# Hybrid encoder layer on one core: where two kinds of work of the recurrence stand (a PSUM bank, and the engine of the set-aside key update)

## Chip, core and metric

The kernel runs on one core of a Trainium2 chip, in float32 throughout. The metric is the device time of one execution in microseconds (us). Engines are named as in the profile: PE (TensorE, with PEld for its weight loads), DVE (VectorE), ACT (ScalarE), POOL (GpSimd) and SP (SyncE, which issues the DMAs).

## What is computed

One encoder layer over 1024 positions of width 1024: a projection into nine parts, a bidirectional gated recurrence (HGRN2) beside a gated spatial mixer, their merge, a SwiGLU feed-forward part and a gated embedding. The change lies in the recurrence. For each of 8 heads (key and value width 128), forward and backward in time, the reference computes

```python
f = lb + (1.0 - lb) * jax.nn.sigmoid(zf)
k = (1.0 - lb) * jax.nn.sigmoid(-zf)
# S_t = diag(f_t) S_{t-1} + k_t v_t^T,   o_t = S_t^T q_t
o = rms_norm(o_fwd + o_bwd, norm_g)
return o * jax.nn.silu(zg)
```

## The kernel before, in words

The layer is a sequence of stages. The stage of the change lies between about 540 and 1040 us of the profiled execution. Before it come the projections that need no recurrence, behind it the merge of both branches, the output projection, the feed-forward part and the gated embedding.

For each head three functions are called. `proj(h)` multiplies the two forget projections (L133, 96 matmuls of 128x512 for each head, in passes of split float32) and makes from them the gates `F` and the keys `X` and `Y` on ACT (L591 to L598), with a clamp on DVE (L599). `scores(h)` builds the 128x128 score blocks within each of the 8 chunks of 128 positions by doubling: seven levels with blocks of m = 1, 2, 4, ..., 64. `outputs(h)` carries the state from chunk to chunk and adds both directions. The loop calls scores(h), then proj(h+1), then outputs(h). Behind the scores of the last head it issues the last gate projections and the loads for the merge, ahead of outputs(7).

Keys of both directions share two tiles. At a level, `X` holds the keys that this level's matmuls use (of one direction in even blocks, of the other in odd ones), and `Y` holds the others, set aside. A level does the following, with g the half of the 1024 positions:

- L624: 4 matmuls (8 PE instructions in the trace) of X against the decayed queries QA into a bank with the tag "sc", for g = 0 and then g = 1.
- L633, `update`: QA of this half is multiplied by gates (DVE, 128x512).
- L636, `update`: half of the new X2 is made as X times gates (DVE, 128x256 for each g).
- L657: the other half of X2 is copied from Y (ACT, 128x512, one for a level).
- L660: the places in Y that were copied are refilled with X times gates (POOL, 128x512, one for a level). The copy of the next level reads what it wrote. **This is the instruction that the change moves.**
- L643 or L646, `merge`: the scores are taken into SC (ACT for m of 32 and 64, under a mask on DVE below that).
- L666: the gates of the next level are products of neighbours (DVE, 128x1024 at m = 1 down to 128x16 at m = 64).

X, Y and F never read a result of PE. Their chain can run ahead of the matmuls as far as the three buffers of X allow, and in the trace it does: when the matmuls of a head are at m = 64, L636, L657 and L660 are at m = 1 and m = 2 of the next head, and L666 is a head ahead.

`outputs(h)` first builds the states. For two groups of chunks (4, then 3) and in each for both directions d (0 forward, 1 backward) it transposes the keys on PE (L683, 4 or 3 of them) into one PSUM bank, copies them to `kt` on ACT (L685, two buffers), multiplies them with the values (L688, bank "st") and adds the products to the running state S on DVE (L692 for the first, L694 for the others). Then, for each half, it sums scores and states into a bank with the tag "o" (L712), normalises (squares at L715 on ACT, a power on POOL at L101, a scaling at L719 on ACT), transposes into the bank "tr" (L722) and multiplies by the gate on DVE (L724).

PSUM has 8 banks: "mm" 3, "sc" 2, and one each of "tr", "st" and "o". So the transposed keys of both directions go through the one bank "tr" before, and each group waits until ACT has copied the one ahead of it. Only backward groups of the last head go to "sc".

The order on each engine's queue is not written out by hand. The kernel is built under `tile.TileContext(nc, schedule_with_timeline_sim=True)`, which orders the instructions of each engine by its own model of their times, and inserts the waits. On the chip the queues are then fixed: an instruction that waits holds up what stands behind it on its engine. So PE interleaves the matmuls of scores(h), outputs(h-1) or outputs(h), and proj(h+1).

Of the kernel before, what the change touches and what calls it, by code (L numbers as in the profile page):

```python
# [22 lines left out]
H = 8  # L23
# [12 lines left out]
def kernel(ctx: ExitStack, tc: tile.TileContext, a: dict, out: bass.AP):  # L36
# [7 lines left out]
    nc = tc.nc  # L44
# [10 lines left out]
    def ps_tile(tag):  # L55
        return psum.tile([P, NH], F32, name=f"ps_{tag}", tag=tag, bufs=PS_BUFS[tag])
# [16 lines left out]
    def t2(pool, role, bufs=2):  # L73
        return pool.tile([P, NH], F32, name=role, tag=role, bufs=bufs)

    def sm(role, w=1):
        return small.tile([P, w], F32, name=role, tag=role)
# [377 lines left out]
    for t in range(NT):  # L455
        tp = ps_tile(("tr", "o")[t % 2])
# [100 lines left out]
    def view(t, off, dims):  # L557
        tv = t[:]
        return bass.AP(tv.tensor, tv.offset + off, [list(tv.ap[0])] + dims)
# [41 lines left out]
    def scores(h, s):  # L601
        q, X, Y, F = s.q, s.X, s.Y, s.F
        QA = hg.tile([P, 2, T], F32, name="QA", bufs=2)
        ks = hg.tile([P, T], F32, name="ks")
        SC = hg.tile([P, NT, P], F32, name="SC", bufs=2)
        nc.vector.tensor_tensor(out=QA, in0=view(q, 0, [[0, 2], [1, T]]), in1=F, op=ALU.mult)
        nc.vector.tensor_tensor(out=ks, in0=X, in1=Y, op=ALU.add)

        for g in range(2):
            sp = ps_tile("sc")  # L610
            for i in range(4):
                cs = slice((4 * g + i) * P, (4 * g + i + 1) * P)
                nc.tensor.matmul(sp[:, i * P:(i + 1) * P], lhsT=ks[:, cs], rhs=q[:, cs], start=True, stop=True)
            nc.scalar.activation(SC[:, 4 * g:4 * g + 4], sp.rearrange("p (c t) -> p c t", c=4), AF.Copy)

        for li, m in enumerate(LEVELS):
            nb = T // m
            cb = P // (2 * m)

            def level(g):  # L620
                sp = ps_tile("sc")
                for i in range(4):
                    c = 4 * g + i
                    nc.tensor.matmul(  # L624
                        sp[:, i * P:(i + 1) * P], lhsT=X[:, c * P:(c + 1) * P],
                        rhs=view(QA, c * P, [[2 * m, cb], [T + m, 2], [1, m]]), start=True, stop=True)
                return sp

            def update(g, X2):

                o, of = g * NH, g * nb // 2
                qd = [[T + m, 2], [2 * m, nb // 4], [1, m]]
                nc.vector.tensor_tensor(out=view(QA, o, qd), in0=view(QA, o, qd),  # L633
                                        in1=view(F, of + 1, [[nb - 1, 2], [2, nb // 4], [0, m]]), op=ALU.mult)
                dims = [[4 * m, nb // 8], [3 * m, 2], [1, m]]
                nc.vector.tensor_tensor(out=view(X2, o, dims), in0=view(X, o, dims),  # L636
                                        in1=view(F, nb + of + 1, [[4, nb // 8], [1 - nb, 2], [0, m]]), op=ALU.mult)

            def merge(g, sp):
                if m >= 32:  # L640
                    for p0 in range(0, P, m):
                        c0 = p0 ^ m
                        nc.scalar.activation(SC[p0:p0 + m, 4 * g:4 * g + 4, c0:c0 + m],  # L643
                                             sp.rearrange("p (c t) -> p c t", c=4)[p0:p0 + m, :, c0:c0 + m], AF.Copy)
                    return
                nc.vector.copy_predicated(  # L646
                    SC[:, 4 * g:4 * g + 4], masks[:, li, None, :].broadcast_to([P, 4, P]),
                    sp.rearrange("p (c t) -> p c t", c=4))

            X2 = hg.tile([P, T], F32, name="X", bufs=3)  # L650
            sp0 = level(0)
            update(0, X2)
            merge(0, sp0)
            sp1 = level(1)

            mid = [[4 * m, nb // 4], [1, 2 * m]]
            nc.scalar.activation(view(X2, m, mid), view(Y, m, mid), AF.Copy)  # L657
            update(1, X2)
            mid = [[4 * m, nb // 4], [m, 2], [1, m]]
            nc.gpsimd.tensor_tensor(out=view(Y, m, mid), in0=view(X, m, mid),  # L660
                                    in1=view(F, 0, [[4, nb // 4], [nb + 3, 2], [0, m]]), op=ALU.mult)
            X = X2
            merge(1, sp1)
            F2 = hg.tile([P, 2, nb // 2], F32, name=f"F{2 * m}", bufs=2 if m == 64 else 1)
            Fv = F.rearrange("p d (b h) -> p d b h", h=2)
            nc.vector.tensor_tensor(out=F2, in0=Fv[:, :, :, 0], in1=Fv[:, :, :, 1], op=ALU.mult)  # L666
            F = F2
        s.QA, s.SC, s.X, s.Y, s.F = QA, SC, X, Y, F

    def outputs(h, s):  # L670
        QA, SC, X, Y, F, v = s.QA, s.SC, s.X, s.Y, s.F, s.v

        S = hg.tile([P, 2, NT - 1, P], F32, name="S")
        orders = [list(range(NT - 1)), list(range(NT - 1, 0, -1))]
        prev = [None, None]
        for g0 in range(0, NT - 1, 4):
            for d in range(2):
                cs = orders[d][g0:g0 + 4]
                n = len(cs)
                tp = ps_tile("sc" if h == H - 1 and d else "tr")  # L680
                for i, c in enumerate(cs):
                    src = X if c % 2 == d else Y
                    nc.tensor.transpose(tp[:, i * P:(i + 1) * P], src[:, c * P:(c + 1) * P], ident)  # L683
                kt = hg.tile([P, 4, P], F32, name="kt", bufs=2)
                nc.scalar.activation(kt[:, 0:n], tp[:, 0:n * P].rearrange("p (c t) -> p c t", c=n), AF.Copy)  # L685
                up = ps_tile("sc" if h == H - 1 and d else "st")
                for i, c in enumerate(cs):
                    nc.tensor.matmul(up[:, i * P:(i + 1) * P], lhsT=kt[:, i], rhs=v[:, c], start=True, stop=True)  # L688
                for i, c in enumerate(cs):
                    uv = up[:, i * P:(i + 1) * P]  # L690
                    if prev[d] is None:
                        nc.vector.tensor_copy(S[:, d, c - d], uv)  # L692
                    else:
                        nc.vector.scalar_tensor_tensor(  # L694
                            out=S[:, d, c - d], in0=S[:, d, prev[d] - d], scalar=F[:, 1 - d, c:c + 1], in1=uv,
                            op0=ALU.mult, op1=ALU.add)
                    prev[d] = c


        for g in range(2):  # L700
            op = ps_tile("sc" if h == H - 1 and g else "o")
            ssq = sm("os", 4)
            for i in range(4):
                c = 4 * g + i
                cs = slice(c * P, (c + 1) * P)
                terms = [(SC[:, c], v[:, c])]
                if c > 0:
                    terms.append((QA[:, 1, cs], S[:, 0, c - 1]))
                if c < NT - 1:
                    terms.append((QA[:, 0, cs], S[:, 1, c]))  # L710
                for j, (l, r) in enumerate(terms):
                    nc.tensor.matmul(op[:, i * P:(i + 1) * P], lhsT=l, rhs=r, start=(j == 0), stop=(j == len(terms) - 1))  # L712
            on = t2(t1, "on")
            for i in range(4):
                nc.scalar.activation(on[:, i * P:(i + 1) * P], op[:, i * P:(i + 1) * P], AF.Square,  # L715
                                     accum_out=ssq[:, i:i + 1])
            r = rstd_from("o", ssq, 4, 1.0 / P)
            for i in range(4):
                nc.scalar.activation(on[:, i * P:(i + 1) * P], op[:, i * P:(i + 1) * P], AF.Identity, scale=r[:, i:i + 1])  # L719
            tp = ps_tile("tr")  # L720
            for i in range(4):
                nc.tensor.transpose(tp[:, i * P:(i + 1) * P], on[:, i * P:(i + 1) * P], ident)  # L722
            gs = slice(g * NH, (g + 1) * NH)
            nc.vector.scalar_tensor_tensor(out=on, in0=tp, scalar=vec[:, 2, h:h + 1], in1=s.zg[:, gs],  # L724
                                           op0=ALU.mult, op1=ALU.mult)
            if h == H - 1:
                A = (A0, A1)[g]
                split_into(A[0][1][:, h % 4, :], A[1][1][:, h % 4, :], on)
            else:
                nc.sync.dma_start(at_d[h, :, gs], on)  # L730
# [363 lines left out]
```

## Time and profile before

| | us |
|---|---|
| median of 3 runs (1967.69 to 1969.16) | 1967.95 |
| profiled execution, its own time | 1966.99 |
| profiled execution, span from first to last instruction | 1965.2 |
| PE busy in the span | 1910.8 |
| DVE, ACT, POOL busy | 1120.0, 757.2, 206.7 |

The profiled execution is 0.96 us below the median, and 1.8 us of it lie outside its span. Matmuls are pipelined and overlap, so a busy time of PE contains the fill of the engine. Idle time of an engine is put down to what ended it last. The granted clock is full (0.997 in the mean) throughout.

### The profile page before, as it was taken

The page shows a single profiled execution, that of the slowest core. Times are in us where ns is not written, and L with a number is a line of the kernel's source. Part 1 is how long each engine was busy: PE and PEld are TensorE (multiplying, and loading weights), DVE is VectorE, ACT ScalarE, POOL GpSimd, SP SyncE. Part 2 cuts the span into 40 slices and gives each one's busy share as a digit, 9 for nine tenths or more (in the row PEclk, how much of TensorE's full clock was granted, in tenths as well). Part 3 has the DMA queues.
Part 4 walks back from the last instruction along what each step waited for, and adds up shares of the span by engine and source line. Part 5 has one row for each costly group of instructions (what it writes and reads, how often), then busy time and mean ns, then how long its engine had stood idle before and what let it go on. Part 6 is the DMA issues. An engine that isn't in the chain of part 4 may idle for free.

```text
span 1965.2 us, 24005 instructions
## 1 busy us (share of the span) xinstructions
PE 1910.8 (97%) x9264; PEld 1596.0 (81%) x9264; DVE 1120.0 (57%) x1712; ACT 757.2 (39%) x1424; POOL 206.7 (11%) x153
## 2 busy tenths in 40 slices
PE   7999999999999999999989998999999999999999
PEld 6887888888887888888877887888888888888887
DVE  7402385544348777777665468855554537545743
ACT  6312254343354545545441356433333324112321
POOL 2600000000012222222112100000000000001000
PEclk9999999999999999999999999999999999999999
DMA  7220245323231221212336333232222106315222
GB/s 292 93 88 27 87 172 170 130 105 110 86 123 33 70 71 63 66 55 68 126 106 208 107 99 103 97 112 78 89 76 86 65 33 209 108 65 163 92 102 79
DMA packets 82690, 201.86 MB, mean 103 GB/s; under 512 B 8720, under 2 KB 18064, under 8 KB 82576
## 3 DMA queue, kind: packets, MB, share of 16 engines
q1 hardware_dynamic: 82576, 200.33, 30.2%
q8 instruction: 73, 1.20, 0.3%
q14 instruction: 41, 0.34, 0.0%
HBM read 147.35 MB, written 52.95 MB: 102 GB/s over the span
## 4 chain that ended last, share of the span: by engine, by line
PE 90%; DVE 4%; ACT 2%; DMA 2%; POOL 1%; issue 1%; SPq 0%; DVEq 0%; POOLq 0%; ACTq 0%
PE ps_mm L133 29%; PE ps_mm L278 20%; PE ps_sc L133 11%; PE ps_sc L278 10%; PE ps_st L133 6%; PE ps_sc L624 4%; PE ps_o L278 2%; PE ps_o L712 2%; PE ps_tr L278 2%; PE ps_st L278 1%; DVE QA L633 1%; POOL Y L660 1%; PE ps_st L688 1%; ACT SC L643 0%; DMA raw<-in_w_gate_dram 0%
## 5 line engine op out<-in xcount | busy, mean ns | idle before, releaser
L278 PE MATMUL ps_mm<-T,w 128*128 128x512 f32 x1296 | 309.6, 389 | 0.0
L278 PEld LDWEIGHTS ps_mm<-T,w 128*128 128x128 f32 x1296 | 243.2, 188 | 50.7 <-ACT u L228 0.2
L115 DVE TENSOR_TENSOR whl<-raw,whl 128x1024 fp32r<-128x1024 f32 (+1 forms) x70 | 89.6, 1282 | 142.7 <-ACT whl L114 142.6
L660 POOL TENSOR_TENSOR Y<-X,F 128x512 f32<-128x512 f32 x56 | 92.4, 1651 | 696.1 <-DVE F L599 392.4
L624 PE MATMUL ps_sc<-QA,X 128*128 128x128 f32 x896 | 126.4, 288 | 16.9 <-DVE QA L633 16.9
L115 DVE TENSOR_TENSOR w<-sums,w 128x1024 fp32r<-128x1024 f32 x72 | 88.0, 1223 | 94.2 <-ACT w L114 94.2
L624 PEld LDWEIGHTS ps_sc<-QA,X 128*128 128x128 f32 x896 | 116.1, 192 | 26.1 <-DVE QA L633 19.0
L133 PE MATMUL ps_mm<-whl,act 128*128 128x512 f32 x528 | 134.1, 389 | 0.0
L114 ACT ACTIVATE whl<-raw 128x1024 fp32r<-128x1024 f32 (+1 forms) x78 | 79.1, 1017 | 120.2 <-PE ps_sc L133 52.4
L633 DVE TENSOR_TENSOR QA<-QA,F 128x512 f32<-128x512 f32 x112 | 91.8, 828 | 49.2 <-PE ps_sc L624 48.1
L133 PE MATMUL ps_mm<-hTb,whl 128*128 128x512 f32 x480 | 118.6, 396 | 0.0
L133 PEld LDWEIGHTS ps_mm<-whl,act 128*128 128x128 f32 x528 | 99.1, 188 | 20.7
L133 PE MATMUL ps_mm<-hTa,whl 128*128 128x512 f32 x480 | 115.1, 392 | 0.0
L114 ACT ACTIVATE w<-sums 128x1024 fp32r<-128x1024 f32 x72 | 75.9, 1055 | 99.9 <-PE ps_sc L278 76.9
L278 PE MATMUL ps_sc<-T,w 128*128 128x512 f32 x432 | 107.5, 389 | 0.0
L133 PEld LDWEIGHTS ps_mm<-hTa,whl 128*128 128x128 f32 x480 | 89.4, 188 | 18.1
L133 PEld LDWEIGHTS ps_mm<-hTb,whl 128*128 128x128 f32 x480 | 88.2, 188 | 16.8
L278 PEld LDWEIGHTS ps_sc<-T,w 128*128 128x128 f32 x432 | 81.1, 188 | 16.9
L133 PE MATMUL ps_sc<-whl,act 128*128 128x512 f32 x354 | 91.0, 390 | 0.3 <-ACT acc L953 0.3
L133 PEld LDWEIGHTS ps_sc<-whl,act 128*128 128x128 f32 x354 | 66.3, 188 | 14.3 <-ACT acc L953 0.7
L115 POOL TENSOR_TENSOR wpg<-raw,wpg 128x1024 fp32r<-128x1024 f32 x4 | 9.6, 2403 | 598.3 <-ACT wpg L114 593.6
L278 PE MATMUL ps_mm<-B,wA 128*128 128x512 f32 x264 | 67.3, 399 | 1.7 <-ACT wA L114 1.7
(309 smaller groups left out, 3574.2 us busy)
## 6 DMA issues: line engine op xcount, KB each, us to landing
raw<-in_w_fm_dram SPq DMA_DIRECT2D x52, 512.0 KB, 3.6
raw<-in_w_gate_dram SPq DMA_DIRECT2D x22, 512.0 KB, 3.4
raw<-in_w_up_dram SPq DMA_DIRECT2D x22, 512.0 KB, 3.9
act_d<-s SPq DMA_DIRECT2D x22, 512.0 KB, 2.8
raw<-in_w_down_dram SPq DMA_DIRECT2D x22, 512.0 KB, 4.4
raw<-act_d SPq DMA_DIRECT2D x22, 512.0 KB, 4.2
raw<-in_w_tm_dram SPq DMA_DIRECT2D x16, 512.0 KB, 4.1
pr_d<-vs SPq DMA_DIRECT2D x16, 256.0 KB, 5.9
```

Source lines behind the costliest of these rows:

```text
L114: nc.scalar.activation(hi, src, AF.Copy)
L115: (eng or nc.vector).tensor_tensor(out=lo, in0=src, in1=hi.bitcast(F32), op=ALU.subtract)
L133: nc.tensor.matmul(ps, lhsT=lhs(lp, k), rhs=rhs(rp, k), start=(i == 0), stop=(i == n - 1))
L278: nc.tensor.matmul(ps, lhsT=lhs(lp, k), rhs=rhs(rp, k), start=(first and i == 0), stop=(i == n - 1), skip_group_check=True)
L624: nc.tensor.matmul(sp[:, i * P:(i + 1) * P], lhsT=X[:, c * P:(c + 1) * P], rhs=view(QA, c * P, [[2 * m, cb], [T + m, 2], [1, m]]), start=T ...
L633: nc.vector.tensor_tensor(out=view(QA, o, qd), in0=view(QA, o, qd), in1=view(F, of + 1, [[nb - 1, 2], [2, nb // 4], [0, m]]), op=ALU.mult)
L660: nc.gpsimd.tensor_tensor(out=view(Y, m, mid), in0=view(X, m, mid), in1=view(F, 0, [[4, nb // 4], [nb + 3, 2], [0, m]]), op=ALU.mult)
L688: nc.tensor.matmul(up[:, i * P:(i + 1) * P], lhsT=kt[:, i], rhs=v[:, c], start=True, stop=True)
L712: nc.tensor.matmul(op[:, i * P:(i + 1) * P], lhsT=l, rhs=r, start=(j == 0), stop=(j == len(terms) - 1))
```

## The change

Two edits. In the level loop of `scores`, the refill of Y (L660) goes from POOL to DVE, with the same operands. In `outputs`, the backward groups of transposed keys (d = 1) go into the bank with the tag "o" in place of "tr"; those of the last head still go to "sc", and forward groups still go to "tr".

```diff
@@ -657,7 +657,7 @@
             nc.scalar.activation(view(X2, m, mid), view(Y, m, mid), AF.Copy)
             update(1, X2)
             mid = [[4 * m, nb // 4], [m, 2], [1, m]]
-            nc.gpsimd.tensor_tensor(out=view(Y, m, mid), in0=view(X, m, mid),
+            nc.vector.tensor_tensor(out=view(Y, m, mid), in0=view(X, m, mid),
                                     in1=view(F, 0, [[4, nb // 4], [nb + 3, 2], [0, m]]), op=ALU.mult)
             X = X2
             merge(1, sp1)
@@ -677,7 +677,7 @@
             for d in range(2):
                 cs = orders[d][g0:g0 + 4]
                 n = len(cs)
-                tp = ps_tile("sc" if h == H - 1 and d else "tr")
+                tp = ps_tile(("tr", "sc" if h == H - 1 else "o")[d])
                 for i, c in enumerate(cs):
                     src = X if c % 2 == d else Y
                     nc.tensor.transpose(tp[:, i * P:(i + 1) * P], src[:, c * P:(c + 1) * P], ident)
```

## Rows read from the trace of the kernel before

**Rows 1.** The page, part 1: busy us, share of the span, instructions.
```profile
PE 1910.8 (97%) x9264; PEld 1596.0 (81%) x9264; DVE 1120.0 (57%) x1712; ACT 757.2 (39%) x1424; POOL 206.7 (11%) x153
```

**Rows 2.** By stretch, one head each: us; busy PE, PEld, DVE, ACT, POOL; clock; DMA.
```profile
573.50:634.00 60.50, 54.94 (x328) 48.24 (x327) 49.68 (x79) 29.80 (x59) 14.26 (x9) 1.00 0.14 44
...
739.50:792.40 52.90, 49.04 (x319) 43.98 (x319) 40.58 (x72) 27.64 (x72) 14.02 (x9) 1.00 0.20 65
...
898.10:955.00 56.90, 56.86 (x349) 50.58 (x350) 45.40 (x72) 32.02 (x75) 11.28 (x8) 1.00 0.31 103
955.00:1020.00 65.00, 57.88 (x376) 51.11 (x376) 36.05 (x69) 23.82 (x79) 10.23 (x9) 1.00 0.26 86
```

**Rows 3.** The same view, inside one head; columns as in rows 2.
```profile
747.00:772.70 25.70, 25.70 (x156) 22.81 (x155) 19.80 (x30) 11.42 (x34) 5.92 (x5) 1.00 0.18 62
772.70:778.10 5.40, 4.49 (x38) 4.05 (x37) 4.54 (x10) 2.83 (x9) 1.18 (x2) 1.00 0.33 100
778.10:782.30 4.20, 4.03 (x34) 3.82 (x35) 4.20 (x10) 3.76 (x11) 2.27 (x1) 1.00 0.58 189
782.30:786.80 4.50, 3.23 (x29) 3.04 (x28) 3.20 (x7) 2.58 (x5) 3.38 (x2) 1.00 0.31 106
```

**Rows 4.** The chain of waits, end of the same head: start us, us, what.
```profile
780.03 4.15 POOL Y L660
...
784.20 0.66 ACT X L657
...
784.88 0.61 ACT kt L685
```

**Rows 5.** Timeline, same head: start us, us, instruction, [idle before <-releaser].
```profile
782.39 1.83 DVE L666 TENSOR_TENSOR F<-F 128x32 f32<-128x32 f32 x1
...
785.53 0.33 PE L683 MATMUL ps_tr<-ident,X 128*128 128x128 f32 x1 [1.27 <-ACT kt L685]
...
790.49 1.28 POOL L660 TENSOR_TENSOR Y<-X,F 128x512 f32<-128x512 f32 x1 [4.05 <-ACT X L657]
...
790.71 1.60 DVE L633 TENSOR_TENSOR QA<-QA,F 128x512 f32<-128x512 f32 x1
...
792.37 1.23 PE L624 MATMUL ps_sc<-QA,X 128*128 128x128 f32 x8 [1.03 <-DVE QA L633]
```

**Rows 6.** Groups by form, DVE from 573.5 to 1020 us: busy us, mean ns | idle.
```profile
L633 DVE TENSOR_TENSOR QA<-QA,F 128x512 f32<-128x512 f32 x112 | 91.8, 828 | 49.2 <-PE ps_sc L624 48.1
L636 DVE TENSOR_TENSOR X<-X,F 128x256 f32<-128x256 f32 x112 | 60.8, 575 | 0.2
...
L666 DVE TENSOR_TENSOR F<-F 128x32 f32<-128x32 f32 x8 | 10.7, 1334 | 0.0
...
L666 DVE TENSOR_TENSOR F<-F 128x64 f32<-128x64 f32 x8 | 1.7, 216 | 0.0
```

**Rows 7.** Instructions of one line, same stretch: duration ns min/median/max.
```profile
L633 DVE TENSOR_TENSOR QA<-QA,F x112: 667/692/2197, 582.7 to 1004.8; 128x512 f32<-128x512 f32 x112
...
L636 DVE TENSOR_TENSOR X<-X,F x112: 400/417/2345, 571.5 to 1001.0; 128x256 f32<-128x256 f32 x112
```

**Rows 8.** Timeline, same head, 776 to 780 us, DVE, PE and ACT.
```profile
776.29 1.00 DVE L636 TENSOR_TENSOR X<-X,F 128x256 f32<-128x256 f32 x2
...
778.90 2.02 PE L624 MATMUL ps_sc<-QA,X 128*128 128x128 f32 x16 [0.17 <-DVE QA L633]
...
779.26 0.69 ACT L657 ACTIVATE X<-Y 128x512 f32<-128x512 f32 x1
```

**Rows 9.** Timeline, first head's end and last head.
```profile
627.26 1.16 PE L688 MATMUL ps_st<-v,kt 128*128 128x128 f32 x8 [1.60 <-DVE S L694]
...
997.33 1.56 DVE L633 TENSOR_TENSOR QA<-QA,F 128x512 f32<-128x512 f32 x1
```

**Rows 10.** Waits of PE, 573 to 1035 us: us in total, times, longest.
```profile
PE ps_tr L683 <- ACT kt L685: 6.5, 5, 1.3
```

**Rows 11.** Timeline: last reader of bank "o" before the keys are transposed.
```profile
772.75 1.14 ACT L719 ACTIVATE on<-ps_o,or 128x128 f32<-128x128 f32 x4 [2.86 <-POOL or L101]
```

## The prediction, made before the change was run

> **What bounds the kernel now.** I read the page first: PE is busy for 97% of the span, DVE for 57% and POOL for 11% [rows 1]. So no engine but PE is short of time over the whole, and an edit that touches neither PE's work nor its waits can be worth at most the 3% in which PE stands idle. Next, the busy time by head [rows 2]. A head from the middle takes 52.90 us, of which PE is busy 49.04: 3.86 us idle. Five heads (634 to 898 us) repeat this row within 0.1 us. The first head has 5.56 us of idle PE, the last 7.12, and the one from 898 to 955 only 0.04, because gate projections fill its holes. The pattern's whole stock of idle PE is thus 5 x 3.86 + 5.56 + 7.12 = 32 us.
>
> Then the inside of one head [rows 3]. Up to 772.7 us projection matmuls cover every wait (25.70 of 25.70 us busy). All the idle time lies in the last 20 us, where the matmuls of levels 16 to 64, the state products, and levels 1 and 2 of the next head have no projections beside them. There PE, DVE and ACT run in turns, and a late instruction on DVE or ACT is paid by PE. In 772.7 to 782.3 DVE is busy 8.74 of 9.6 us: nearly full.
>
> The chain of waits shows which late instruction that is [rows 4]. The refill of Y at level 1 sits on POOL for 4.15 us; the copy L657 of level 2 waits for it, and holds up ACT's queue, in which the copy of the transposed backward keys (L685) stands behind it. PE waits for that copy: 1.27 us ahead of L683 at 785.53 [rows 5].
>
> The second cost is less visible. At 790.49 a refill begins on POOL, at 790.71 a QA update on DVE, and the update takes 1.60 us [rows 5] where the median of its line is 0.69 [rows 7]. It ends 0.54 us behind the POOL instruction, as if it had first waited for it. L666 at 782.39, a product of 32 elements, takes 1.83 us and ends 0.04 us after POOL is done with the 4.15 us refill [rows 4, 5]; the form of 64 elements has a mean of 0.216 us [rows 6]. So POOL's and DVE's products with two SBUF inputs shut each other out here, and both lose. The Trainium skill (SBUF — State Buffer, "Who interferes with whom") gives this as a rule: a DVE instruction with two SBUF inputs contends with a GpSimd instruction that reads SBUF, and the loser blocks fully; these rows agree. Reckoned without such a lock, the edit would add the whole 38.8 us below to DVE and give it nothing back.
>
> **The change, part by part.** *Refill on DVE, the engine's load.* Added: 7 levels x 8 heads = 56 products of 128x512 from SBUF. The nearest row is L633, same shape, same kind of strided view: 692 ns median [rows 7]. 56 x 0.692 = 38.8 us, 4.8 for a head. The bounds are 0.667, its least, and 0.828, its mean with POOL in the way [rows 6, 7]. Removed: what POOL's refills cost DVE. L633: (828 - 692) x 112 = 15.2 us. L636: (575 - 417) x 112 = 17.7. L666 with 32 elements: (1334 - 216) x 8 = 8.9. Together 41.8 us [rows 6, 7]. So DVE's load hardly changes (some 3 us less), and POOL keeps only the 16 power instructions, as far as this stage goes. What counts is where on the queue the 0.69 us falls.
>
> *Steady head, gains.* The refill of level 1 takes 0.69 in place of 4.15 us. It can start on DVE behind the copy of level 1, which ends at 779.95 [rows 8]; L657 of level 2, at 784.20 before [rows 4], can then follow from 780.7 on, and L685 behind it. The PE wait of 1.27 us goes. What is late next there is L613, the first matmuls of the next scores: PE's own work. The QA update at 790.71 loses its lock: 1.60 - 0.69 = 0.91 of the 1.03 us that PE waits for it [rows 5].
>
> *Steady head, losses.* The refill of level 64 now stands on DVE around 776, ahead of the QA update for which level 64 on PE waits already (0.17 us [rows 8]). It adds 0.69, and the two L636 at 776.29 fall from 1.00 to about 0.75 (2 x 417 ns, less an overlap of 0.08): 0.44 us lost. The refill of level 4 becomes ready at about 790.4, just as the QA update does at 790.71; behind it on the queue it costs nothing, ahead of it up to 0.69. I take half, 0.35. The refills of levels 2, 8, 16 and 32 cost nothing here: for the last three, projections cover PE (25.70 of 25.70 [rows 3]), and at level 2 DVE has 1.3 us idle in its stretch (3.20 of 4.50 [rows 3]). Without that cover each would cost 0.69. While a refill waits for its copy on ACT, the updates behind it on DVE wait too, up to the copy's 0.69 us; the two L636 of the same level take as long, so I take nothing, and keep 0.69 for the bound.
>
> Per head 1.27 + 0.91 - 0.44 - 0.35 = 1.4 us. The wait for L685 occurs 5 times [rows 10]: 7.0 us.
>
> *First and last head.* At 627.26 PE waits 1.60 us for a state update on DVE [rows 9], behind products that POOL holds up; I give back 1.60 and the same 0.91, less 0.44 and 0.35: 1.7. In the last head the QA update at 997.33 takes 1.56 [rows 9]; 0.87 back, less 0.44: 0.4.
>
> *Backward keys in bank "o".* Same transposes, same copies, no instruction more. It lifts one order: the backward group needs no longer wait until ACT has emptied "tr" of the forward group, and the second forward group no longer waits for the backward copy. The bank is free: its last reader, L719, ends at 773.9 [rows 11], 7 us before the backward group runs. The next user of "o" is the output sum, the bulk of which is only due late in the next head; its two early matmuls move behind the second copy, at no cost. By itself the edit shifts the 1.27 us wait from L683 to the product L688 just behind it, which needs that same `kt`; I put 0 on it, between 0 and the 1.27 already counted. No DMA is added or moved and nothing is queued on SP; POOL's queue loses the 56 refills.
>
> *Sum.* 7.0 + 1.7 + 0.4 = 9.1 us. From the profiled execution's 1966.99: 1957.9; it lies 0.96 under the median of 1967.95, so against the runs shown 1958.9, rounded to 1959.
>
> **The rivals.** *A, the holes close almost wholly.* With ACT and DVE sooner, everything in the last 20 us moves up, and the scheduler places projection matmuls in what is left. The stock of the five steady heads is 19.3 us; with 1.7 from the first that is 21: 1947. For it: the head at 898 has 0.04 us idle with enough filler. Against it: between the matmuls of levels 1 and 2 a QA update of 0.69 stands each time, and the filler is spent by then.
>
> *B, the wait is replaced.* PE's 1.27 us goes, but the level's next matmuls then stand for the same QA updates, or for a bank "sc" that ACT empties; what is won at the start is waited for again. For it: the 1.03 and 0.17 us waits show the chain through DVE is as tight as that through ACT [rows 5, 8]. Gain 0 to 3 us: 1966. That the change doesn't do what it says belongs here too: if POOL's lock isn't what stretches DVE, its load rises by 38.8 us, but a gain of 1.27 x 5 against 0.44 and 0.69 x 5 remains, about zero.
>
> *C, slower: DVE's queue becomes the bound in the tight stretch.* Its place is 772.7 to 792.4, where DVE has 0.9 us free in the first 9.6. The four refills there (levels 64, 1, 2, 4) take 4 x 0.69 = 2.8 us, and each may first stand for its copy on ACT, half of 0.69 in the middle: 1.4. Returned are 1.27 + 0.91 + 0.25 = 2.4. Net 1.8 a head, over 7 heads 12 us: 1980. It decides as soon as more than 2.4 us of refills and their waits stand ahead of what PE needs. For it: queues are fixed when the program is built, and a refill waits on a third engine. Against it: DVE gets back as much time as it takes on, and three of the four have room. The Trainium skill (Perfetto Trace Analysis, "Optimizing Scalar/DVE Operations") says that where DVE is saturated it may make sense to offload to GpSimd; that rule speaks against the change and by it the time would be C's. The same section adds that the two share a port, so it might not help.
>
> **How the numbers follow.** A measurement of this kernel can tell about 0.2% (4 us) from no change. My forecast has 0.55, A 0.10, B 0.16, C 0.19. So faster 0.65 (forecast and A), within 0.2% 0.16, slower 0.19. The range runs from A's 1947 to 1976, between no change and C's 1980: it leaves out some gains beyond A and the worse half of C. The forecast's own range is 1951 (no losses: 2.18 x 5 + 2.5 + 0.9 = 14 us, and some of A) to 1964 (every loss in full).
>
> **What would show it.** Right: no POOL instruction but L101 in the heads; L633 at a mean near 0.70 and L636 near 0.42; the moved product near 0.69; DVE's busy time in a steady head within 1 us of 40.6; L657 of level 2 no longer released by the refill late; heads of about 51.5 us with some 2.5 us of idle PE. Wrong: heads at 52.9 with a new wait ahead of L624 or L688 (B); DVE idle ahead of the refill until L657, and PE's waits for L633 grown past 2 us a head (C); or a stage behind this one whose order, and time, has moved.

## The result, and the profile after

The changed kernel takes 2012.25 us (median of 5 runs, 2011.02 to 2013.09) beside 1969.05 for the kernel before in the same series: 43.2 us more, a ratio of 1.022 (95% interval 1.0206 to 1.0234). The prediction said 1959 and a range up to 1976: wrong in sign and outside the range.

The page's part 1 of the changed kernel [rows 1]:

```profile
PE 1934.7 (96%) x9264; PEld 1615.3 (80%) x9264; DVE 1114.4 (55%) x1768; ACT 759.1 (38%) x1424; POOL 114.4 (6%) x97
```

POOL lost its 56 refills, and DVE, which took them, is busy 5.6 us **less** than before. By form on DVE, from 573.5 to 1064 us (busy us, mean ns | idle before) [rows 6]:

```profile
L633 DVE TENSOR_TENSOR QA<-QA,F 128x512 f32<-128x512 f32 x112 | 76.0, 687 | 60.4 <-PE ps_sc L624 60.0
L636 DVE TENSOR_TENSOR X<-X,F 128x256 f32<-128x256 f32 x112 | 46.1, 447 | 0.1
L660 DVE TENSOR_TENSOR Y<-X,F 128x512 f32<-128x512 f32 x56 | 41.7, 745 | 0.8 <-ACT X L657 0.7
...
L666 DVE TENSOR_TENSOR F<-F 128x32 f32<-128x32 f32 x8 | 1.5, 182 | 0.0
```

So what the prediction said of the operations came about: L633 has a mean of 687 ns where it had 828, L636 447 where it had 575, the 32-element product 182 where it had 1334. No engine got more to do, and yet PE lost time. By stretch (us; busy PE, PEld, DVE, ACT, POOL; clock; DMA) [rows 2], with two whole heads counted from one head's output sums to the next:

```profile
779.98:839.91 59.93, 51.58 (x319) 45.43 (x319) 40.26 (x79) 27.72 (x71) 2.01 (x2) 0.97 0.17 58
839.91:901.41 61.50, 53.13 (x318) 46.98 (x318) 40.27 (x79) 27.72 (x71) 2.01 (x2) 0.94 0.17 56
...
785.47:788.90 3.43, 3.43 (x16) 3.20 (x17) 0.75 (x1) 0.72 (x3) 0.00 (x0) 0.52 0.16 60
788.90:790.20 1.30, 1.29 (x12) 1.10 (x10) 0.00 (x0) 0.20 (x1) 0.00 (x0) 1.00 0.11 43
```

From head 2 on, such a head takes 60 to 62 us in place of 52.9. In the first of these two, PE is idle for 59.93 - 51.58 = 8.35 us, where a steady head had 3.86 [rows 2], and busy 2.5 us longer for the same matmuls. PE's waits from 528 to 1080 us (us in total, times, longest) show which idle time is new [rows 10] (before, L722 waited once, for 2.9 us, and L624 for L633 16.9 us in 25 places):

```profile
PE ps_tr L722 <- ACT on L719: 15.0, 5, 3.0
PE ps_sc L624 <- DVE QA L633: 13.6, 13, 3.0
PE ps_sc L624 <- DVE ov L99: 8.6, 4, 2.5
PE ps_o L712 <- DVE S L694: 6.3, 3, 2.1
```

L683's wait for `kt`, 6.5 us in 5 heads before, is gone as predicted. New are waits around the **output sums** L712 of an earlier head, which the prediction left where they were. The timeline of PE and DVE in one head shows their place (start us, us, instruction, [idle before <-releaser]) [rows 5]:

```profile
769.53 1.18 PE L133 MATMUL ps_mm<-hTa,whl 128*128 128x512 f32 x4
...
775.85 2.05 PE L613 MATMUL ps_sc<-q,ks 128*128 128x128 f32 x16
779.98 0.49 PE L712 MATMUL ps_o<-S,QA 128*128 128x128 f32 x2 [2.08 <-DVE S L694]
...
785.47 1.25 PE L722 MATMUL ps_tr<-ident,on 128*128 128x128 f32 x4 [2.99 <-ACT on L719]
...
786.94 1.06 PE L712 MATMUL ps_o<-S,QA 128*128 128x128 f32 x4
...
789.13 0.61 PE L712 MATMUL ps_o<-S,QA 128*128 128x128 f32 x4
...
790.23 2.29 DVE L606 TENSOR_TENSOR QA<-q,F 128x2048 f32<-128x2048 f32 x1 [2.72 <-PE ps_o L712]
...
792.66 1.56 PE L624 MATMUL ps_sc<-QA,X 128*128 128x128 f32 x8 [2.48 <-DVE ov L99]
```

The last four projection matmuls stand at 769.53. The sums, but for an early pair, come behind all 96 of them, even behind L613 of the next scores, and nothing is left to put beside them. So their whole chain lies open: half the sums, squares on ACT, the power on POOL, scaling on ACT, the transposes, the other half. Then DVE can make the next QA (L606), because its buffer is the one that these sums read, and only then can level 1 of the next head begin. The label "DVE ov L99" names the last event ahead of L624; L99 takes 0.16 us behind L606, which took the 2.29. The chain of waits has the same steps (start us, us, what) [rows 4]:

```profile
779.98 2.51 PE ps_o L712 x20
...
784.01 1.02 POOL or L101
...
786.72 3.49 PE ps_o L712 x22
...
790.23 1.95 DVE QA L606
```

For a head that is 2.08 + 2.99 + 2.48 = 7.55 us of new idle time, 7.55 of the 8.35; the old waits are down to 0.8, for the projections now lie where they were. Of the 2.5 us of longer busy time, some 1.6 belong to the clock, which was 0.52 in the 3.43 us behind the gap at L722 (3.43 x 0.48) and 1.00 again behind that: four sum matmuls take 1.06 us at 786.94 and 0.61 at 789.13.

Over the whole span (of the profiled execution, 2013.09 us, the longest of the five) the loss has two halves. PE is idle for 2011.2 - 1934.7 = 76.5 us, 22.1 more than before (1965.2 - 1910.8 = 54.4). And it is busy 23.9 us longer for the same 9264 matmuls. The mean granted clock is 0.985 against 0.997; an estimate from these means puts the clock that was lost at 0.015 x 2011.2 = 30 us against 0.003 x 1965.2 = 6. By this estimate most of the longer busy time is matmuls at the lower clock. The second of the two heads has more of it, with a clock of 0.94 over the whole head, and already behind its first gap, again 2.08 us long:

```profile
839.91:843.00 3.09, 3.09 (x14) 3.09 (x15) 0.15 (x1) 0.00 (x0) 0.00 (x0) 0.50 0.00 0
```

### The profile page after: what moved, and what is told of

Read it like the earlier page. It is cut to its first block, busy times and chain, and to the rows that moved or that the text cites. A ratio compares the mean times of both kernels' runs of the same rounds, so it can differ in the third digit from the quotient of the medians.

```text
span 2011.2 us, 23958 instructions
## 1 busy us (share of the span) xinstructions
PE 1934.7 (96%) x9264; PEld 1615.3 (80%) x9264; DVE 1114.4 (55%) x1768; ACT 759.1 (38%) x1424; POOL 114.4 (6%) x97
## 4 chain that ended last, share of the span: by engine, by line
PE 89%; DVE 6%; DMA 2%; ACT 1%; issue 1%; POOL 0%; SPq 0%; DVEq 0%; POOLq 0%; ACTq 0%
PE ps_mm L133 29%; PE ps_mm L278 19%; PE ps_sc L133 11%; PE ps_sc L278 10%; PE ps_st L133 6%; PE ps_sc L624 4%; PE ps_o L712 2%; PE ps_o L278 2%; PE ps_tr L278 1%; DVE QA L633 1%; PE ps_st L278 1%; DMA xt<-in_x_dram 1%; PE ps_st L688 1%; DVE X L636 1%; DVE Y L660 1%
## 5 line engine op out<-in xcount | busy, mean ns | idle before, releaser
L115 DVE TENSOR_TENSOR whl<-raw,whl 128x1024 fp32r<-128x1024 f32 (+1 forms) x70 | 85.4, 1222 | 132.9 <-ACT whl L114 132.9
L624 PE MATMUL ps_sc<-QA,X 128*128 128x128 f32 x896 | 128.6, 295 | 24.0 <-DVE QA L633 13.6
L624 PEld LDWEIGHTS ps_sc<-QA,X 128*128 128x128 f32 x896 | 118.7, 199 | 31.4 <-DVE QA L633 9.8
L633 DVE TENSOR_TENSOR QA<-QA,F 128x512 f32<-128x512 f32 x112 | 76.0, 687 | 60.4 <-PE ps_sc L624 60.0
L133 PEld LDWEIGHTS ps_mm<-hTb,whl 128*128 128x128 f32 x480 | 88.7, 188 | 17.3
L278 PEld LDWEIGHTS ps_sc<-T,w 128*128 128x128 f32 x432 | 81.1, 188 | 16.8
L101 POOL TENSOR_TENSOR or<-ov,expo 128x4 f32<-128x4 f32 x16 | 18.1, 1128 | 865.9 <-DVE ov L99 865.9
L278 PE MATMUL ps_sc<-B,w 128*128 128x512 f32 x264 | 65.6, 390 | 0.7 <-ACT w L114 0.7
```

The source lines that it names most:

```text
L101: nc.gpsimd.tensor_tensor(out=r, in0=v, in1=expo[:, 0:w], op=ALU.pow)
L115: (eng or nc.vector).tensor_tensor(out=lo, in0=src, in1=hi.bitcast(F32), op=ALU.subtract)
L133: nc.tensor.matmul(ps, lhsT=lhs(lp, k), rhs=rhs(rp, k), start=(i == 0), stop=(i == n - 1))
L278: nc.tensor.matmul(ps, lhsT=lhs(lp, k), rhs=rhs(rp, k), start=(first and i == 0), stop=(i == n - 1), skip_group_check=True)
L624: nc.tensor.matmul(sp[:, i * P:(i + 1) * P], lhsT=X[:, c * P:(c + 1) * P], rhs=view(QA, c * P, [[2 * m, cb], [T + m, 2], [1, m]]), start=T ...
```

## The experiments

The theory from this trace: **the order.** The planner that builds the queues has put the output sums elsewhere. It orders by its own model of times, and the two edits change what that model starts from; its estimates were not looked at. The rivals are the engine (DVE can't carry the refills) and the bank (keys and sums get in each other's way in "o"). The start of the main block of sums, head by head, read from each timeline (us; the last column is the last sum matmul of the stage):

| kernel | head 0 | 1 | 2 | 3 | 4 | last sum |
|---|---|---|---|---|---|---|
| before | 647.9 | 700.7 | 753.6 | 806.4 | 859.3 | 1014.7 |
| after | 657.0 | 717.4 | 780.0 | 839.9 | 901.4 | 1058.7 |
| whole change, order pinned | 651.2 | 703.2 | 755.2 | 807.1 | 859.1 | 1012.4 |
| refill on DVE, order pinned | 652.4 | 704.1 | 755.8 | 807.5 | 859.1 | 1014.9 |

In the changed kernel the sums of heads 0 and 1 are late for another reason: more matmuls stand ahead of them (from 540 us to head 2's sums 1337 instructions of PE, against 1192), and up to there PE idles no longer than before (13.5 us against 13.2). The chain lies open from head 2 on.

The kernel before ran at 1968.42 us in the series of 1, 2 and the first run of 4, at 1968.48 in that of 3, the last run of 4 and the first of 5, and at 1969.08 in that of the other two.

**1. Each edit alone.** First only the engine:

```diff
-            nc.gpsimd.tensor_tensor(out=view(Y, m, mid), in0=view(X, m, mid),
+            nc.vector.tensor_tensor(out=view(Y, m, mid), in0=view(X, m, mid),
```

> The refill of Y on DVE alone, bank tr as before. In this program the order of PE is no longer that of before: from the third head on, the output sums of a head (L712) stand behind all projections of the head after. Order theory (the time is lost because the sums have no projections beside them any more): slower than before, 1990 to 2025 us, with heads of 56 to 62 us and PE idle around L712. Engine theory (the refills themselves are too much for DVE's queue): about the 2012 us of the whole change as well, but with the waits ahead of L633 and L636. Bank theory (the shared bank o is the cause): at or below before, 1955 to 1970.

Measured: 1985.11 us, ratio 1.0085 (1.007 to 1.010). As in the whole change the sums stand behind the last projections (those end at 774.6), and their chain lies open. The time is under the 1990 us from which the order theory's range starts; the direction and the place of the waits came. PE's idle time over the span is only 3.3 us more than before (57.7 us), and its busy time 15.6 us more (1926.4), at a mean clock of 0.988: more of this loss is matmuls that take longer than idle time. The timeline:

```profile
777.31 0.39 PE L712 MATMUL ps_o<-S,QA 128*128 128x128 f32 x2
...
782.71 1.10 PE L722 MATMUL ps_tr<-ident,on 128*128 128x128 f32 x4 [2.10 <-ACT on L719]
...
788.74 1.55 PE L624 MATMUL ps_sc<-QA,X 128*128 128x128 f32 x8 [2.47 <-DVE ov L99]
```

Then only the bank, the refill on POOL:

```diff
-                tp = ps_tile("sc" if h == H - 1 and d else "tr")
+                tp = ps_tile(("tr", "sc" if h == H - 1 else "o")[d])
```

> The backward keys in bank o alone, the refill on POOL as before. The order of PE keeps the period of before, head by head, with the sums between the projections. Order theory: 1960 to 1970, near before. Engine theory: the same. Bank theory: about 2012.

Measured: 1979.96 us, ratio 1.0061 (1.0044 to 1.0078), so this expectation failed: an edit that the prediction put at 0 costs 11.5 us alone. Here the sums stay between the projections; the loss has another place. PE's waits, 573 to 1035 us:

```profile
PE ps_st L688 <- DVE S L694: 21.8, 6, 4.0
```

No transposes wait any more, so PE reaches the backward product L688 sooner, and that must have the bank "st" of the forward one, which DVE empties with its state updates (see 4). PE's idle time over the span grows by only 5.6 us, for other waits shrink; its busy time grows by 7.2 (1918.0). The two edits alone add 16.7 + 11.5 = 28 us; together they cost 43, so they aren't two prices that add.

**2. The whole change, the order held.** One edge that carries no data says that the first matmul of level 1 is queued on PE behind the last L688 of the first backward group of the head before:

```diff
+    marks, gates = {}, {(1, 0): (0, 1)}
+    def behind(ins, mark):
+        tc.add_manual_dep(ins.ins, marks[mark].ins.name, mybir.DependencyInfo(mybir.DependencyClass.NoSync, mybir.DependencyReason.DATA), reason="order")
...
+                    if i == 0 and gates.get((m, g)) in marks: behind(mmi, gates[m, g])
...
+                    marks[g0, d] = nc.tensor.matmul(up[:, i * P:(i + 1) * P], lhsT=kt[:, i], rhs=v[:, c], start=True, stop=True)
```

> The whole change, and one edge of issue order without a wait: the first matmul of level 1 of a head is queued on PE behind the last state product of the first backward group of the head before. That alone gives back the order of before (sums between the projections), with every refill on DVE and the backward keys in bank o. Order theory: 1948 to 1962, the gain that the prediction summed (7 to 20 us). Engine theory: stays above 2000, since DVE has the same work. Bank theory: stays above 2000 too.

Measured: 1964.82 us (10 runs), ratio 0.9981 (0.9972 to 0.9991). All instructions of the change are there, on the same engines and in the same banks, and 47 us are gone. The engine and the bank as causes of the 43 us fall. The time lies above the 1948 to 1962 of the order theory too: the order gives back the loss, and less than half of the gain that was summed. The timeline has the sums between projections again:

```profile
801.01 5.39 PE L133 MATMUL ps_mm<-hTa,whl 128*128 128x512 f32 x23
...
807.12 0.39 PE L712 MATMUL ps_o<-S,QA 128*128 128x128 f32 x2
...
810.49 5.16 PE L133 MATMUL ps_mm<-hTb,whl 128*128 128x512 f32 x22
```

The head is 51.96 us long, 0.89 less than before. Its busy times and clock, and PE's waits from 528 to 1080 us:

```profile
755.16:807.12 51.96, 49.72 (x320) 44.17 (x319) 40.17 (x79) 27.41 (x71) 3.96 (x2) 1.00 0.20 65
```

```profile
PE ps_sc L624 <- DVE QA L633: 7.7, 10, 2.1
PE ps_o L712 <- ACT kt L685: 5.6, 5, 1.1
...
PE ps_tr L683 <- DVE Y L660: 1.3, 5, 0.3
```

The 1.27 us wait for `kt` [rows 5, 10] has gone from the transposes and come back as 1.1 us ahead of the early output sum, which shares the bank "o" with the backward keys.

**3. A few refills decide the order.** Without any edge, the whole change with one level's refill back on POOL (8 of 56):

```diff
-            nc.vector.tensor_tensor(out=view(Y, m, mid), in0=view(X, m, mid),
+            (nc.gpsimd if m == 2 else nc.vector).tensor_tensor(out=view(Y, m, mid), in0=view(X, m, mid),
```

> The whole change, except that the refill of level 2 (8 of the 56 refills of key sets) stays on POOL. Nothing is pinned, yet with this the program queues PE's work as in the pinned run: the output sums between the projections. Order theory: as the pinned run, 1960 to 1972 us, although 48 of the 56 moved refills and the bank edit stand as in the changed kernel; the head period is 52 to 52.5 us, a little over the pinned run's 51.95 for the lock of one POOL refill on DVE (0.2 to 0.9 us a head). Engine theory (DVE carries too much with the refills): 48/56 of the +43 us stays, so about 2005 us. Bank theory (the keys in the bank of the outputs cost it): about 2012 us, since that edit is whole.

Measured: 1967.69 us, ratio 0.9995 (0.9986 to 1.0005). That is 44.6 us below the whole change: all of its loss. And from the other side, the kernel before with only level 1's 8 refills on DVE:

```diff
-            nc.gpsimd.tensor_tensor(out=view(Y, m, mid), in0=view(X, m, mid),
+            (nc.vector if m == 1 else nc.gpsimd).tensor_tensor(out=view(Y, m, mid), in0=view(X, m, mid),
```

> The kernel before with only the refill of level 1 (8 of 56) on DVE, nothing else. With it the program queues the output sums behind later projections and levels than in the kernel before. Order theory: slower, 1975 to 1995 us, though the longest POOL refill (4.15 us) and its wait are gone and only 8 x 0.7 us of work has come to DVE. Engine theory: 8 refills of 56 are too few to matter, and the wait of 1.27 us a head is shorter: 1960 to 1969 us.

Measured: 1991.49 us, ratio 1.0114 (1.0099 to 1.0129). Eight short instructions, and the sums stand behind the projections again (the last of those end at 770.9); from its timeline:

```profile
772.30 0.39 PE L712 MATMUL ps_o<-S,QA 128*128 128x128 f32 x2
...
787.44 1.56 PE L624 MATMUL ps_sc<-QA,X 128*128 128x128 f32 x8 [1.72 <-DVE ov L99]
```

The size of the edit does not set the size of the loss here. The times of both runs came as the order theory said.

**4. What the bank edit costs alone.** Bank "o", with level 1's refill alone on DVE ("e2" in the expectation is the bank edit alone, from 1):

```diff
-            nc.gpsimd.tensor_tensor(out=view(Y, m, mid), in0=view(X, m, mid),
+            (nc.vector if m == 1 else nc.gpsimd).tensor_tensor(out=view(Y, m, mid), in0=view(X, m, mid),
...
-                tp = ps_tile("sc" if h == H - 1 and d else "tr")
+                tp = ps_tile(("tr", "sc" if h == H - 1 else "o")[d])
```

> Bank o, and of the refills only that of level 1 (8 of 56) on DVE, the others on POOL. The order of PE is that of e2. Order theory: the 4.15 us refill on the chain is gone, 1.3 us a head less than in e2 and perhaps the first head's 1.6: 1953 to 1962. Engine theory: a seventh of the loss, about 1972. Bank theory: about 2012.

Measured: 1978.60 us, ratio 1.0049 (1.0034 to 1.0064). Missed: the longest refill is off POOL, and the wait for "st" is still 19.3 us in 6 places. The timeline:

```profile
785.15 2.02 PE L624 MATMUL ps_sc<-QA,X 128*128 128x128 f32 x16 [0.16 <-DVE QA L633]
787.01 1.06 PE L688 MATMUL ps_st<-v,kt 128*128 128x128 f32 x8
...
789.88 1.28 DVE L666 TENSOR_TENSOR F<-F 128x32 f32<-128x32 f32 x1
...
792.02 1.20 DVE L666 TENSOR_TENSOR F<-F 128x16 f32<-128x16 f32 x1
793.14 0.72 DVE L694 SCALAR_TENSOR_TENSOR S<-S,F,ps_st 128x128 f32<-128x128 f32 x2
...
793.91 1.16 PE L688 MATMUL ps_st<-v,kt 128*128 128x128 f32 x8 [3.41 <-DVE S L694]
```

Two products that take 0.18 and 0.17 us in the changed kernel take 1.28 and 1.20 beside refills on POOL, with the last state updates behind them. That suggested the lock as the cause, and a test with two other levels' refills on DVE (16 of 56) and that of level 1 back on POOL:

```diff
-            nc.vector.tensor_tensor(out=view(Y, m, mid), in0=view(X, m, mid),
+            (nc.vector if m >= 32 else nc.gpsimd).tensor_tensor(out=view(Y, m, mid), in0=view(X, m, mid),
```

> The bank edit, with the refills of levels 32 and 64 alone on DVE (16 of 56); the other 40 stay on POOL, the 4.15 us one of level 1 among them. Nothing is pinned; the program queues PE's work in the order of the pinned run. It asks why the bank edit alone cost 11.5 us: PE then waited 3.4 to 3.9 us in each head for the bank of the state products, which DVE's state updates free, and DVE's halving of the decays for levels 32 and 64, in front of those updates, took 1.28 and 1.20 us beside a POOL refill against 0.18 and 0.16 with the refills on DVE. Lock theory: with those two refills on DVE the wait is gone or under 1 us a head, and the time is 1962 to 1969 us though 40 refills are still on POOL. Rival (the bank edit itself costs, or the POOL refill of level 1 does): it stays at 1976 to 1982 us, as the bank edit alone and the one with only level 1 on DVE.

Measured: 1977.79 us, ratio 1.0050 (1.0035 to 1.0065). The expected time failed. The wait for "st" did fall, to one of 3.6 us, and four heads (704.0 to 915.3 us) have a mean of 52.8 where the bank edit alone had 54.9. But the reason in the expectation is wrong too. The refills that collide in the timeline above belong to levels 2 and 4 of the next head, and here they are still on POOL:

```profile
784.30 1.16 PE L688 MATMUL ps_st<-v,kt 128*128 128x128 f32 x8 [0.25 <-ACT kt L685]
...
787.37 0.33 DVE L694 SCALAR_TENSOR_TENSOR S<-S,F,ps_st 128x128 f32<-128x128 f32 x1
...
788.29 1.56 POOL L660 TENSOR_TENSOR Y<-X,F 128x512 f32<-128x512 f32 x1 [1.40 <-ACT X L657]
...
788.63 1.06 PE L688 MATMUL ps_st<-v,kt 128*128 128x128 f32 x8
...
1045.95 1.22 PE L133 MATMUL ps_mm<-A,whl 128*128 128x512 f32 x2 [5.69 <-ACT whl L114]
```

What differs is once more the order. Here, as in the pinned run, the first product comes behind 8 of the level matmuls, with the other 8 behind it, and all four updates stand on DVE ahead of the products that POOL can hold up; in the bank edit alone and with level 1 on DVE it comes behind all 16. The time that the heads give back is lost elsewhere, and not in waiting: PE's idle time over the span is 54.6 us, as before (54.4), and it is busy 10.5 us longer for the same matmuls, at a mean clock of 0.991 against 0.997:

```profile
PE 1921.3 (97%) x9264; PEld 1604.7 (81%) x9264; DVE 1108.8 (56%) x1728; ACT 756.4 (38%) x1424; POOL 186.4 (9%) x137
```

The last sums start 4.2 us later than in the kernel before (1018.9 against 1014.7), 3.8 of it from head 0 already, which has the one wait of 3.6 us; and at 1045.95 the merge stands 5.69 us for a weight tile. Why that tile is late was not tested.

That the order and not the lock makes the wait for "st", a run shows in which POOL has no refill at all. It was meant for something else, to queue the early sum of run 2 later by a second edge:

```diff
+                    marks["o"] = nc.tensor.matmul(op[:, i * P:(i + 1) * P], lhsT=l, rhs=r, start=(j == 0), stop=(j == len(terms) - 1)); g + i + j or behind(marks["o"], (4, 1))
```

> The pinned run with a second order edge: the first matmul of the output sums is queued on PE behind the last backward state product of its head, instead of between two groups of level-1 matmuls, where it waited 1.1 us in 5 heads for ACT's copy of the backward keys out of the bank that both now use. If that wait was on the path that sets the end, 5 us go: 1957 to 1961 us, below both kernels. If PE's next wait (for the level's queries and keys from DVE) takes it up, 1963 to 1967 us and the waits of level matmuls for DVE grow by about the same 5 us.

Measured: 1985.38 us, ratio 1.0079 (1.0059 to 1.0098); both expectations failed. The second edge moved more than the sum: the first product is again behind 16 level matmuls (787.64), and the wait for "st" is back, 17.3 us in 6 places:

```profile
787.64 2.02 PE L624 MATMUL ps_sc<-QA,X 128*128 128x128 f32 x16
789.67 1.16 PE L688 MATMUL ps_st<-v,kt 128*128 128x128 f32 x8
...
796.15 1.16 PE L688 MATMUL ps_st<-v,kt 128*128 128x128 f32 x8 [2.88 <-DVE S L694]
```

2.88 us without a lock, 3.41 and up to 4.0 with one: that fits a lock that adds to the wait, but the lock doesn't make it.

**5. What is left when the order is held.** Refill on DVE and the edge of 2, the keys left in bank "tr" (the diffs of the engine and of the edge together):

> All 56 refills on DVE, the key transposes left in their old bank, and the one order edge of the pinned run. This gives the price of the bank edit in the good order, by comparison with the pinned run (1964.8 us), and of the order alone by comparison with the refill on DVE without the edge (1985.1 us). Order theory: 1955 to 1968 us; without the bank edit the early sum no longer waits for the copy of the backward keys (1.1 us a head, 5 heads), but the keys' transposes wait for the copy before them again (1.27 us a head), so within 4 us of the pinned run. Engine theory: as the run without the edge, 1985 us.

Measured: 1964.07 us, ratio 0.9972 (0.9963 to 0.9982), the lowest median of the study. Against the refill on DVE alone (1985.11) one edge gives 21 us. Against the whole change in the held order (1964.82) the bank edit is worth nothing that can be measured (0.7 us). Against the expectation no transposes wait for `kt`, though the old bank serves both directions:

```profile
PE ps_sc L624 <- DVE QA L633: 12.3, 21, 2.1
...
PE ps_tr L683 <- DVE Y L660: 1.0, 5, 0.2
```

The 1.1 us wait of the early sum in run 2 can be taken away without a second edge: with the edge of 2 kept, only the first group of backward keys goes into bank "o".

```diff
+                tp = ps_tile(("tr", "sc" if h == H - 1 else ("o" if g0 == 0 else "tr"))[d])
```

> The pinned run with only the first of the two groups of backward keys of a head in the bank of the head outputs; the second goes back to the bank of the transposes, so that the early output sum need not wait for its copy (1.1 us in 5 heads of the pinned run). If that wait is on the path: 1957 to 1961 us. If PE only moves it to the waits for the level's queries and keys from DVE, as the run with refills on DVE, the pin and no bank edit suggests (1964.1 us without that wait): 1962 to 1966 us, with the level matmuls' waits for DVE up by 4 to 5 us from 7.7.

Measured: 1966.12 us, ratio 0.9986 (0.9977 to 0.9995). This is the second of the two cases, 0.1 us above its range. The early sum waits no more, and PE stands for DVE instead, 16.8 us where it was 7.7, twice the rise that was expected:

```profile
PE ps_sc L624 <- DVE QA L633: 16.8, 15, 2.1
```

## Why the prediction was wrong

**The step that failed** is the one under all the others. It costed the edits within the queues of the trace of before: the gains were read "at 785.53" and "at 790.71", and of the output sums it said that "the bulk of which is only due late in the next head". That needs an order that stays. Here the planner orders every queue anew, and an edit changes what it takes as its start. The text named "a stage behind this one whose order, and time, has moved" as a way to be wrong, but gave it no chance and no price, and not the heads themselves. The runs of 2 and 3 give the price: 47 us by one edge, 44.6 by 8 refills. Which estimate of the planner tips the sums over is open.

**A second term stood at nothing: PE's busy time.** The sum took 9.1 us of idle time away and left the busy time as it was. In the held order (below, run 2 is the whole change with its edge, run 5 the refill on DVE with it) the idle time did go, 7.1 us in run 2 and 8.7 in run 5, but the busy time for the same matmuls grew by 4.1 and 7.9, and the medians gained 3.6 and 4.4 us. The profiled run of run 5 is the slowest of its ten, 2.1 us above the median.

```profile
PE 1914.9 (98%) x9264; PEld 1599.4 (82%) x9264; DVE 1112.8 (57%) x1768; ACT 757.2 (39%) x1424; POOL 117.7 (6%) x97
PE 1918.7 (98%) x9264; PEld 1602.4 (82%) x9264; DVE 1112.4 (57%) x1768; ACT 758.3 (39%) x1424; POOL 118.7 (6%) x97
```

Part of it is the clock, 0.996 and 0.994 in the mean against 0.997; what makes the rest is open.

**The lock of POOL and DVE** was right. The rows show 687, 447 and 182 ns against 692, 417 and 216 expected. From 540 us to 65.3 us behind the last sum's start, DVE's busy time fell by 2.0 us (374.3 against 376.3) where 3 was said; the rest of the 5.6 lies in stages that the change doesn't touch. The rule cited from the Trainium skill (SBUF — State Buffer, "Who interferes with whom") agrees with these rows, and the first timeline of 4 shows it once more: 1.28 against 0.18 us. The moved product was put at 0.69; its least and median are close to that, but at level 1 it takes 1.12, so its mean is 745 ns.

**The steady head**, judged in the pinned runs, where the order is that of before in the places costed: 1.4 us of gain were forecast, heads of about 51.5 with 2.5 us of idle PE. Measured: 51.96 with 51.96 - 49.72 = 2.24 idle, a gain of 0.89 (run 2), and 51.70 with 2.47 idle (run 5), a gain of 1.15 without the bank edit. So the idle time came out as forecast; run 2's head is busy 0.7 us longer than before, at a clock of 1.00. The bank's 0 came out in the time (run 2 against run 5), though not as reasoned: "at no cost" was said of the early sums, and their wait is 1.1 us a head. Without that edit the 1.27 us goes too, by the refill alone. Alone, the bank edit costs 11.5 us, by an order again (4). **The first head** did not give the 1.7: its sums start 3.3 us later in run 2, not sooner. There the first state product stands behind all 16 level matmuls, as with the bank edit alone (4); the wait for the state update, 1.60 us before, is 2.88 at 630.58, and behind it the clock was 0.73 and 0.70 in two stretches of 3 us.

**Rival B**, 1966, is close to what the change is worth in a held order (1964.8): the wait replaced, at L712 and then at DVE (the last run of 5). **Rival C**, 1980, had the sign but not the mechanism: DVE's queue didn't become the bound, and run 5 with all 56 refills on DVE is faster than the kernel before. The rule for C, from the Trainium skill (Perfetto Trace Analysis, "Optimizing Scalar/DVE Operations"), gets no support here: DVE is at 57% over the span, and in the stage it is busy 2.0 us less with 56 more instructions. **Rival A**, 1947, fails: heads with a stock of 3.86 us got shorter by at most 1.15.

## What to carry to other kernels

Where a planner orders the queues, a small edit is two changes: its own, which the trace prices, and a new order, which it doesn't. Compare the place of the large blocks on the busiest engine first, before any duration, and if they have moved, hold the order by an edge and measure the edit by itself. Then read the busy time of that engine beside its idle time: here half of the loss was the same matmuls taking longer. A forecast for such a kernel needs a case for "the order moves", sized by the longest chain that now hides beside other work: here sums, power, scaling, transposes and the next QA.

## What the runs showed of the hardware

Behind the gap of 2.99 us in which PE stood ahead of L722, the granted clock was 0.52 for 3.43 us, about the lower of TensorE's two levels (1.2 of 2.4 GHz), then 1.00 again. Behind the gaps of 2.08 and 2.48 us in the same head it stayed at 1.00, but in the next head it was 0.50 for 3.09 us behind a gap of the same 2.08 us: the length of one gap doesn't decide it. The kernel before isn't at full clock throughout either: from 1020 to 1023 us, behind waits of 2.92 and 0.94 us, it was 0.51. In a head of the pinned run, where PE's longest wait is 1.1 us, it was 1.00 throughout. So a wait can cost more than its length: by the estimate above the first stretch lost some 1.6 us on top of the 2.99.

A DVE product of 128x512 from SBUF depends on its view: the refill takes 1.12 us at level 1 and 0.68 at the median, the same number of elements.
